# Moving the sums of w_out's features into the late local attention, and tying V's transposes to the next strip

## The chip, the cores and the metric

The kernel runs on one core of a Trainium2 chip. A core has five engines that each take their own instructions in order and wait for one another through semaphores: TensorE (PE, matrix products; its weight loads, PEld, overlap its products), VectorE (DVE), ScalarE (ACT), GpSimd (POOL) and SyncE (SP), which in this kernel issues every DMA. The metric is the device time of one execution in microseconds (us). Three executions of the kernel before gave 2171.97, 2172.36 and 2172.82 us; their median is 2172.36 us.

## The reference, cut to what matters

One encoder layer over two requests (a prompt of 1024 tokens, a sample of 256), each with 16 learned meta tokens in front:

```python
u = rms_norm(h, norm_w) @ w_in              # 2048 -> 6656 features
qa, ka, va, za, qb, kb, vb, zb = jnp.split(u, split_points(), axis=-1)
ya = global_gqa(rope(norm(qa)), rope(norm(ka)), va) * silu(za)      # 8 heads, 2 groups of K and V
yb = neighbourhood_attention(norm(qb), norm(kb), vb, rpb) * silu(zb)  # 8 local heads, 8 x 16 window
y = concatenate([ya, yb]) @ w_out           # 2048 -> 2048
return h + y
```

All is float32. A float32 product is made of three products in the type fp32r: a number is split into a high part h and a remainder l, and h·h, h·l and l·h are added.

## The kernel before

**Two chunks of tokens.** `chunk1` projects 512 tokens (the sample, the first 240 prompt tokens and the meta tokens) and runs the sample's attention. `chunk2` projects the other 784 prompt tokens in two blocks of 512 and 272 columns and runs the prompt's attention. `outproj` then multiplies with `w_out`.

**Strips.** w_in is cut into 52 strips of 128 features: Q, K, V and Z of the global heads and of the local heads. `project` takes one to three strips, `strips` (lines 184 to 227) runs them: for each of four quarters `c` of the 2048 input features it loads a piece of weights `wr` (line 196), splits it into `wh` on ACT and `wl` on DVE (lines 65 and 66), and runs for each block `b` of tokens 4 × 3 matmuls (lines 217 to 219). In `chunk2`, strips not named in `AGAIN` load their `wl` from HBM, where `chunk1` left it; the local heads 4 to 7 split again. When a strip is done, its `evac` brings it out of PSUM and norms it: K and Q through `qk_evac`, Z through `z_evac`, V through `v_rows` (line 279) and then transposes on PE against an identity (`v_turn`, line 286; `rows_out`, line 530), whose results ACT copies out of the only PSUM tile `tp` and SP stores to HBM (`vn`).

**Order.** The instructions are traced by the program and then placed on each engine's queue by a scheduler that follows a simulated timeline; on the chip each queue runs in just that order. `add_manual_dep(a, b.name, NoSync)` only puts `a` behind `b` in that order, and `issue_after(b)` does so for all instructions of a block on `b`'s engine. `turn_ins` (line 229) collects transposes in the list `turned`; in the kernel before only those of `chunk1`'s last V strip are put behind a matmul, the last of the first quarter and block of `chunk2`.

**Places.** After each odd quarter of a strip, `run_due` (line 233) takes the next entry of the list `due`. In `chunk2`, the first 8 local strips are spread over the global heads; the other 24 run after them and give 48 places (`LATE`), into which `local_heads` (line 899) puts the loads, the `scores` and, two places later, the `values` of the local heads 0 to 6; the last strip is local head 7's Z, and head 7's attention runs in the first places of `outproj`. Before the last strip, `turn` reverses the order of its blocks.

**Sums of w_out.** `outproj` multiplies by a scheme with seven products of halves of y and w_out instead of eight (Strassen's, in Winograd's form), which needs four sums of w_out's quarters. `w_sums` (line 579) is a generator with 16 rounds of two steps: step one loads four tiles `wq` of 128 × 512 from w_out (line 593), step two makes four differences on DVE (line 586, put behind the last split of weights) and stores them to `td` in HBM (line 603). `project` takes a step for each strip of `chunk1` from the 21st on. The tiles come from the pool `xr` (10 buffers), which also holds x while it is loaded. `outproj` reads `td` for its third product and later (line 1008).

**The passage from chunk1 to chunk2.** `load_all_x` (line 141) loads the x of `chunk2` into 16 tiles `xb` and 16 tiles `xa` (line 161, tile name `x`), which lie where `chunk1` had its own x; ACT and DVE scale and split them (lines 162 and 163). The last Q strip's store `qfd` (line 647) stands on SP's queue among these loads.

Of the kernel before, what the change touches and what calls it, by code (L numbers as in the profile page):

```python
# [12 lines left out]
F32 = mybir.dt.float32  # L13
# [8 lines left out]
P = 128  # L22
DM = 2048
KT = 16
# [34 lines left out]
class Kern:  # L59
# [88 lines left out]
    def load_all_x(self):  # L148


        nc, self.xload = self.nc, {}
        for kt in range(KT):
            w = self.nw[:, kt:kt + 1]
            self.xs[kt] = []
            ta = self.x.tile([P, 2, NB], F32R, tag="xa", name="x", align_bytes=ALIGN)
            tb = self.xb.tile([P, NX], F32R, tag="xb", name="xb", align_bytes=ALIGN)
            o = 0
            for h, l in ((ta[:, 0], ta[:, 1]), (tb[:, :NT2], tb[:, NX - NT2:])):
                r, n = l.bitcast(F32), l.shape[1]
                with self.tc.issue_after(self.early):  # L160
                    self.xload.setdefault(kt, nc.sync.dma_start(r, self.x2d[kt][:, o:o + n]).ins)
                nc.scalar.activation(h, r, AF.Copy, scale=w)
                nc.vector.scalar_tensor_tensor(out=l, in0=r, scalar=w, in1=h.bitcast(F32), op0=ALU.mult, op1=ALU.subtract)
                self.xs[kt].append((h, l))
                o += n
        self.behind = [None] + [self.xload[c] for c in range(WCH - 1, KT, WCH)]
        for d, c in self.consts:
            with self.tc.issue_after(self.xload[KT - 1]):
                nc.sync.dma_start(d, c)
# [12 lines left out]
    def strips(self, jobs, getx):  # L182


        nc, tc = self.nc, self.tc
        out = [[pool.tile([P, 512], F32, tag=tag, name="pp") for pool, tag in pools] for _, _, pools in jobs]
        for c in range(KT // WCH):
            ws = []
            behind = self.behind.pop(0) if self.behind else None
            for j, (s, _, _) in enumerate(jobs):  # L190
                wp = self.w if j < 2 else self.w1
                with tc.high_priority(offset=self.woff), tc.issue_after(behind) if behind else nullcontext():
                    w = self.raw.tile([P, WCH, P], F32, tag="raw", name="wr")
                    cuts = ((0, 1), (1, WCH)) if self.projected == 3 and c == 0 and not self.second else ((0, WCH),)
                    for i, e in cuts:
                        self.lastw = nc.sync.dma_start(w[:, i:e], self.io["w_in"][s][:, c * WCH + i:c * WCH + e, :]).ins
                    wh = wp.tile([P, WCH, P], F32R, tag="wh", name="wh")
                    wl = wp.tile([P, WCH, P], F32R, tag="wl", name="wl")
                    if self.second and s not in AGAIN:
                        nc.sync.dma_start(wl[:].bitcast(F32), self.wld[s][:, c * WCH:(c + 1) * WCH, :])  # L200
                        nc.scalar.copy(wh[:], w[:])
                    else:
                        for i, e in cuts:
                            self.lastsplit = self.split(wh[:, i:e], wl[:, i:e], w[:, i:e])
                            self.lasthi = self.hi
                ws.append((wh, wl))
                if not self.second and s not in AGAIN:
                    nc.sync.dma_start(self.wld[s][:, c * WCH:(c + 1) * WCH, :], wl[:].bitcast(F32))
            nb = len(jobs[0][1])
            for b in range(nb)[::-1] if self.turn else range(nb):  # L210
                for k in range(WCH):
                    kt = c * WCH + k
                    xh, xl = getx(kt)[b]
                    first, last = kt == 0, kt == KT - 1
                    for (wh, wl), ps, (_, blocks, _) in zip(ws, out, jobs):
                        p, n = ps[b], blocks[b][1]
                        nc.tensor.matmul(p[:, :n], wh[:, k, :], xh[:, :n], start=first, stop=False)  # L217
                        nc.tensor.matmul(p[:, :n], wh[:, k, :], xl[:, :n], start=False, stop=False)  # L218
                        self.lastmm = nc.tensor.matmul(p[:, :n], wl[:, k, :], xh[:, :n], start=False, stop=last).ins  # L219
                if self.second and self.turned:  # L220
                    for i in self.turned:
                        tc.add_manual_dep(i, self.lastmm.name, mybir.DependencyInfo(
                            mybir.DependencyClass.NoSync, mybir.DependencyReason.DATA), reason="turned")
                    self.turned = None
            if c % 2:
                self.run_due()
        return out

    def turn_ins(self, i):
        if not self.second:  # L230
            self.turned.append(i)

    def run_due(self):
        if self.late:
# [327 lines left out]
    def project(self, *parts):  # L562

        if not self.second:
            self.projected += len(parts)
            if self.projected > 20:
                for _ in range(len(parts)):
                    next(self.sums, None)
            kt = self.projected - 33
            for i in [i for i in self.xsq if i < kt]:  # L570
                self.square_x2(i, self.xsq.pop(i))
            if 0 <= kt < KT:
                with self.tc.issue_after(self.lastw):
                    self.xsq[kt] = self.load_x2(kt)
            if self.projected == 48:
                self.early = self.lastw
        jobs = [(p[0], p[1], [p[3] if len(p) > 3 else (self.pp, "pp")] * len(p[1])) for p in parts]
        out = self.strips(jobs, self.xs.__getitem__ if self.second else self.get_x)
        return [p[2](ps) for p, ps in zip(parts, out)]

    def w_sums(self):

        nc, w = self.nc, self.io["w_out"]

        def sub(out, a, b):
            nc.vector.tensor_tensor(out=out, in0=a, in1=b, op=ALU.subtract)

        for k in range(8):
            for o in range(0, FH, FB):
                q = {}  # L590
                for n, j, c in (("12", k, FH + o), ("11", k, o), ("22", 8 + k, FH + o), ("21", 8 + k, o)):
                    r = self.xr.tile([P, FB], F32, tag="xr", name="wq")
                    nc.sync.dma_start(r[:], w[:, j, c:c + FB])
                    q[n] = r[:]
                yield

                with self.tc.issue_after(self.lastsplit):
                    sub(q["11"], q["12"], q["11"])
                    sub(q["12"], q["22"], q["12"])
                    sub(q["22"], q["22"], q["11"])  # L600
                    sub(q["21"], q["22"], q["21"])
                for n, p in (("11", 5), ("12", 7), ("22", 6), ("21", 4)):
                    nc.sync.dma_start(self.td[p][:, k, o:o + FB], q[n])
                yield

    def chunk1(self):
        nc, io = self.nc, self.io
        self.early_due, self.place = {}, 0
        self.due, self.late, self.turn, self.behind, self.turned = iter(()), [], False, [], []
        self.woff, self.second, self.projected, self.sums = 0, False, 0, self.w_sums()  # L610
        self.scale2 = [self.one2.tile([P, T2], F32, tag=n, name=n) for n in ("rb2", "eb2")]
        self.xsq = {}
# [27 lines left out]
        def qb_strip(s, h, wc):  # L640
# [3 lines left out]
            def evac(ps):  # L644
                o, n = BQ
                self.qk_evac(ps[0], o, n, wc, None, [], q[:, :n])
                nc.sync.dma_start(self.qfd[h][:], q[:, NS:n])
                return q[:, :NS]
            return s, [BQ], evac

# [80 lines left out]
        for h in range(8):  # L731
# [9 lines left out]
                got["v"], = pr(vj)  # L741
                pr(zj)
            else:
                self.turned = []
                v, z = pr(v_strip(VB + h, 2 + h), z_strip(ZB + h, 8 + h))
                for _ in run(8 + h, q, z, k, *v, self.bias_table(h, "bs", (2 * HALF,))[:]):
                    pass
# [2 lines left out]
    def chunk2(self):  # L750
# [7 lines left out]
        self.consts = [(ct, io["ropec"][:, T1:]), (st, io["ropes"][:, T1:])]  # L758
        self.load_all_x()
        BL = [(0, NB), (NB, T2 - NB)]  # L760

        def k_first(g):
            t = self.k.tile([P, 2 * NP + 2 * NMETA], F32R, tag="k1", name="kf", align_bytes=ALIGN)
# [134 lines left out]

        def local_heads():
            places = [[] for _ in range(LATE)]  # L900
            seq = (values, load_v, load_z, scores, load_kq)

            def put(n, f, *a):
                places[n].append((seq.index(f), f, a))
# [1 line left out]
            for h in range(NH - 1):  # L906
# [4 lines left out]
                if h + 2 < NH:  # L911
                    put(max(o + 3, 8 * h - 2), load_kq, h + 1)
                    put(max(o + 5, 8 * h), load_v, h + 1)
                    put(max(o + 5, 8 * h), load_z, h + 1)
            put(LATE - 4, load_kq, NH - 1)
            put(LATE - 2, load_v, NH - 1)
            return [sorted(p, key=lambda x: x[0]) for p in places]

# [12 lines left out]
        for g in range(2):  # L931
            if g == 0:
                k, _ = pr(k_strip(KA, 0, kw, True), v_rows_of(VA, 0))
            else:
                k, = pr(k_strip(KA + g, g, kw, True))
                pr(v_rows_of(VA + g, g))
# [8 lines left out]
            f(0)  # L945
        self.due = iter(local_heads())
        fill(len(late) - 1)
        self.turn = True
        fill(1)
        load_z(NH - 1)  # L950
        self.due = iter([[(0, f, (NH - 1, b)) for f, b in ((values, n - 2), (scores, n)) if 0 <= b < 4] for n in range(6)])
# [360 lines left out]
```

## Time and profile before

| | |
|---|---|
| median of three executions | 2172.36 us |
| the profiled execution | 2171.32 us |
| its span, first to last instruction | 2169.5 us |
| ACT busy | 1119.3 us, 52% |
| POOL busy | 516.4 us, 24% |
| moved by DMA | 383.83 MB, 177 GB/s over the span |
| `chunk1`, by the first and last of its matmuls | to about 609 us |
| first score of the late local attention; end of the last strip | 1325.4 us; 1774.6 us |

An engine is busy while one of its instructions runs. Matmuls overlap: two matmuls of 128 × 512 start 0.23 us apart, though each is shown with 0.39 us. A row of the view of groups or of the timeline gives line, engine, operation and tiles as out<-in, and in brackets the idle time of the engine just before, with what ended it. A row of the view of waits reads: engine, tile, line <- what it waited for: us in total, times, the longest. A row of the view by stretches gives the stretch's length and, for each engine, busy time and count, then TensorE's granted clock as a share of full speed, the DMA engines' busy share and GB/s.

### The profile page before, as it was taken

How to read it: one execution, taken by the hardware profiler on the slowest of the kernel's cores; microseconds unless marked ns; L12 is line 12 of the kernel's file. 1: busy time of each engine (PE TensorE's matmuls, PEld its weight loads, DVE VectorE, ACT ScalarE, POOL GpSimd, SP SyncE). 2: the span in 40 equal slices, each digit the busy share in tenths (PEclk: the TensorE clock that was granted, in tenths of full speed). 3: DMA queues.
4: the chain of work that ended last, by engine and by line, in shares of the span. 5: the costliest groups of instructions: out<-in, count | busy, mean ns of one | idle time of the engine just before them, and what ended most of it. 6: DMA issues, size and time to landing. Idle time of an engine off the chain costs nothing. (4 is left out here: it accounts for less than half of the span.)

```text
span 2169.5 us, 34094 instructions
## 1 busy us (share of the span) xinstructions
PE 2155.3 (99%) x11745; PEld 1877.3 (87%) x11745; DVE 1644.9 (76%) x2989; ACT 1119.3 (52%) x2291; POOL 516.4 (24%) x250
## 2 busy tenths in 40 slices
PE   9999999999999999999999999999999999999999
PEld 7888878888888999999999999898999888888887
DVE  7787886777874899987799988677787876545763
ACT  6555544555554676665666765444443454232230
POOL 1232331221311233322143314333333311000000
PEclk9999999999999999999999999999999999999999
DMA  8767798988654333334333344554433364662663
GB/s 300 223 203 227 237 307 302 339 277 270 214 191 148 100 105 113 118 110 142 100 107 109 105 129 151 184 156 138 135 127 119 113 206 147 238 227 99 233 223 107
DMA packets 263182, 383.83 MB, mean 177 GB/s; under 512 B 44992, under 2 KB 112992, under 8 KB 263008
## 3 DMA queue, kind: packets, MB, share of 16 engines
q1 hardware_dynamic: 263008, 381.65, 53.8%
q8 instruction: 92, 1.51, 0.3%
q14 instruction: 82, 0.67, 0.1%
HBM read 281.01 MB, written 100.38 MB: 176 GB/s over the span
## 5 line engine op out<-in xcount | busy, mean ns | idle before, releaser
L217 PE MATMUL pp<-x,wh 128*128 128x512 f32 (+1 forms) x1664 | 654.8, 395 | 2.7 <-ACT wh L65 1.6
L219 PE MATMUL pp<-x,wl 128*128 128x512 f32 (+1 forms) x1664 | 649.4, 391 | 1.1 <-DVE wl L66 1.1
L218 PE MATMUL pp<-x,wh 128*128 128x512 f32 (+1 forms) x1664 | 648.9, 390 | 0.0
L219 PEld LDWEIGHTS pp<-x,wl 128*128 128x128 f32 x1664 | 313.0, 188 | 63.1 <-DVE wl L66 2.4
L217 PEld LDWEIGHTS pp<-x,wh 128*128 128x128 f32 x1664 | 312.8, 188 | 59.7 <-ACT wh L65 3.9
L218 PEld LDWEIGHTS pp<-x,wh 128*128 128x128 f32 x1664 | 313.2, 188 | 52.6
L253 POOL PARTITION_ALL_REDUCE m<-ms x78 | 224.1, 2873 | 408.4 <-ACT ms L251 400.4
L66 DVE TENSOR_TENSOR wl<-wr,wh 128x512 fp32r<-128x512 f32 (+2 forms) x287 | 219.2, 766 | 112.9 <-ACT wh L65 102.2
L336 POOL PARTITION_ALL_REDUCE tot<-a x80 | 182.4, 2280 | 451.2 <-DVE a L333 451.2
L65 ACT CAST wh<-wr 128x512 fp32r<-128x512 f32 (+2 forms) x287 | 174.2, 611 | 201.9 <-PE pp L218 177.2
L218 PE MATMUL pp<-xb,wh 128*128 128x272 f32 x832 | 240.1, 289 | 0.0
L219 PE MATMUL pp<-xb,wl 128*128 128x272 f32 x832 | 239.6, 288 | 0.0
L217 PE MATMUL pp<-xb,wh 128*128 128x272 f32 x832 | 239.6, 288 | 0.0
L1036 PE MATMUL pq<-wm,yh 128*128 128x512 f32 x560 | 218.6, 390 | 0.0
L1037 PE MATMUL pq<-wm,yh 128*128 128x512 f32 x560 | 218.0, 389 | 0.0
L1038 PE MATMUL pq<-wm,yl 128*128 128x512 f32 x560 | 217.9, 389 | 0.0
L318 POOL PARTITION_ALL_REDUCE ma<-m x80 | 103.3, 1291 | 400.2 <-DVE m L316 399.7
L217 PEld LDWEIGHTS pp<-xb,wh 128*128 128x128 f32 x832 | 156.5, 188 | 7.4
L218 PEld LDWEIGHTS pp<-xb,wh 128*128 128x128 f32 x832 | 156.4, 188 | 7.4
L219 PEld LDWEIGHTS pp<-xb,wl 128*128 128x128 f32 x832 | 157.3, 189 | 0.3
L1038 PEld LDWEIGHTS pq<-wm,yl 128*128 128x128 f32 x560 | 105.1, 188 | 22.0
L1036 PEld LDWEIGHTS pq<-wm,yh 128*128 128x128 f32 x560 | 105.1, 188 | 21.6
(211 smaller groups left out, 3835.3 us busy)
## 6 DMA issues: line engine op xcount, KB each, us to landing
wr<-in_w_in SPq DMA_DIRECT2D x413, 256.0 KB, 3.5
wld<-wl SPq DMA_DIRECT2D x132, 256.0 KB, 4.2
wl<-wld SPq DMA_DIRECT2D x132, 256.0 KB, 3.2
yr<-yd SPq DMA_DIRECT2D x35, 512.0 KB, 5.5
wq<-in_w_out SPq DMA_DIRECT2D x64, 256.0 KB, 5.0
td<-wq SPq DMA_DIRECT2D x64, 256.0 KB, 4.4
ww<-td SPq DMA_DIRECT2D x64, 256.0 KB, 5.4
ww<-in_w_out SPq DMA_DIRECT2D x48, 256.0 KB, 4.5
```

Source lines behind the costliest of these rows:

```text
L65: self.hi = nc.scalar.copy(hi, full).ins
L66: return nc.vector.tensor_tensor(out=lo, in0=full, in1=hi.bitcast(F32), op=ALU.subtract).ins
L217: nc.tensor.matmul(p[:, :n], wh[:, k, :], xh[:, :n], start=first, stop=False)
L218: nc.tensor.matmul(p[:, :n], wh[:, k, :], xl[:, :n], start=False, stop=False)
L219: self.lastmm = nc.tensor.matmul(p[:, :n], wl[:, k, :], xh[:, :n], start=False, stop=last).ins
L253: nc.gpsimd.partition_all_reduce(m2[:], ms[:], P, RED.add)
L318: nc.gpsimd.partition_all_reduce(ma[:], m1[:], P, RED.max)
L336: nc.gpsimd.partition_all_reduce(tot[:], a1[:], P, RED.add)
L1036: nc.tensor.matmul(ps, yh, wh, start=k == 0, stop=False)
L1037: nc.tensor.matmul(ps, yh, wl, start=False, stop=False)
L1038: self.lastmm = nc.tensor.matmul(ps, yl, wh, start=False, stop=k == 7).ins
```

## The change

Three things change. The 32 steps of `w_sums` leave `project` and go into the places 6 to 37 of the late local attention, last in each place, and their tiles come from the pool `ph` (tags `ph` and `pl`, two buffers each), which the global attention used for its probabilities. All transposes of V, in both chunks, are put behind a matmul of the next strip: the last one of the quarter and block that `tie` names, (1, 0) in `chunk1`, (0, 0) at `chunk2`'s start, (0, 1) after its first project and (1, 0) in its last strip. And the store `qfd` of `chunk1`'s last Q strip is put behind the load of x's ninth tile on SP's queue.

```diff
@@ load_all_x
+        self.tc.add_manual_dep(self.qstore, self.xload[KT // 2].name, mybir.DependencyInfo(
+            mybir.DependencyClass.NoSync, mybir.DependencyReason.DATA), reason="x first")
         self.behind = [None] + [self.xload[c] for c in range(WCH - 1, KT, WCH)]
@@ strips
-                if self.second and self.turned:
+                if self.turned and (c, b) == self.tie:
                     for i in self.turned:
                         tc.add_manual_dep(i, self.lastmm.name, mybir.DependencyInfo(
                             mybir.DependencyClass.NoSync, mybir.DependencyReason.DATA), reason="turned")
-                    self.turned = None
+                    self.turned = []
...
     def turn_ins(self, i):
-        if not self.second:
-            self.turned.append(i)
+        self.turned.append(i)
@@ project
             self.projected += len(parts)
-            if self.projected > 20:
-                for _ in range(len(parts)):
-                    next(self.sums, None)
@@ w_sums
-                    r = self.xr.tile([P, FB], F32, tag="xr", name="wq")
+                    r = self.ph.tile([P, FB], F32, tag="ph" if n in ("12", "22") else "pl", name="wq", align_bytes=ALIGN)
                     nc.sync.dma_start(r[:], w[:, j, c:c + FB])
@@ chunk1
-        self.due, self.late, self.turn, self.behind, self.turned = iter(()), [], False, [], []
+        self.due, self.late, self.turn, self.behind, self.turned, self.tie = iter(()), [], False, [], [], (1, 0)
...
-                nc.sync.dma_start(self.qfd[h][:], q[:, NS:n])
+                self.qstore = nc.sync.dma_start(self.qfd[h][:], q[:, NS:n]).ins
...
-                self.turned = []
                 v, z = pr(v_strip(VB + h, 2 + h), z_strip(ZB + h, 8 + h))
@@ chunk2
         BL = [(0, NB), (NB, T2 - NB)]
+        self.tie = 0, 0
...
-            seq = (values, load_v, load_z, scores, load_kq)
+            seq = (values, load_v, load_z, scores, load_kq, next)
...
             put(LATE - 4, load_kq, NH - 1)
+            for n in range(32):
+                put(6 + n, next, self.sums)
...
                 k, _ = pr(k_strip(KA, 0, kw, True), v_rows_of(VA, 0))
+                self.tie = 0, 1
...
-        self.turn = True
+        self.turn, self.tie = True, (1, 0)
         fill(1)
```

## The prediction

> **What bounds the kernel now.** I read the page's head first, then the view of waits for PE, then busy time by stretches.
>
> ```profile
> span 2169.5 us, 34094 instructions
> PE 2155.3 (99%) x11745; PEld 1877.3 (87%) x11745; DVE 1644.9 (76%) x2989; ACT 1119.3 (52%) x2291; POOL 516.4 (24%) x250
> ...
> PE tp L530 <- DVE vt L279: 2.9, 2, 2.5
> ...
> PE tp L286 <- DVE vt L279: 1.3, 1, 1.3
> ...
> PE pp L219 <- DVE wl L66: 1.1, 2, 0.6
> PE pp L217 <- ACT x L162: 1.1, 1, 1.1
> PE po L408 <- ACT ph L65: 1.1, 2, 0.5
> ```
>
> PE is busy for all but 2169.5 − 2155.3 = 14.2 us, and the change gives PE not one matmul more or less. So no faster engine elsewhere can help: the change can only win what PE stands idle or slowed, and can only lose by making it wait anew. The stretches say where it stands.
>
> ```profile
> 216.00:285.00 69.00, 65.44 (x307) 53.42 (x307) 59.95 (x104) 36.82 (x76) 27.52 (x10) 1.00 0.75 245
> 285.00:600.00 315.00, 315.00 (x1428) 260.40 (x1428) 243.26 (x410) 160.11 (x325) 74.55 (x29) 1.00 0.85 282
> 600.00:625.00 25.00, 23.92 (x119) 19.47 (x118) 22.81 (x42) 17.41 (x35) 3.22 (x2) 1.00 0.70 248
> 705.00:1340.00 635.00, 635.00 (x4115) 581.40 (x4114) 560.62 (x1022) 423.98 (x866) 187.70 (x91) 1.00 0.36 113
> 1359.00:1680.00 321.00, 320.87 (x1925) 289.15 (x1924) 244.02 (x522) 143.60 (x329) 111.68 (x59) 1.00 0.45 144
> 1761.60:1765.10 3.50, 3.50 (x11) 2.76 (x10) 1.69 (x3) 1.46 (x4) 0.00 (x0) 0.51 0.78 253
> ```
>
> Three spots stand out: 216 to 285 (idle 69.00 − 65.44 = 3.56 us), the passage to chunk 2 (25.00 − 23.92 = 1.08 us), and about 1752 to 1765, where the two waits of `tp` L530 sum to 2.9 us and the granted clock then falls to 0.51.
>
> **The last strip (V's tie).** The transposes of the last V strip stand early in the last Z strip.
>
> ```profile
> 1753.34 0.32 SPq L856 DMA_DIRECT2D qfull<-q2d  x1
> ...
> 1756.87 1.05 ACT L65 CAST q<-qfull 128x1024 fp32r<-128x1024 f32 x1 [2.00 <-DMA vm<-vmd]
> ...
> 1757.95 1.23 DVE L66 TENSOR_TENSOR q<-qfull,q 128x1024 fp32r<-128x1024 f32 x1 [2.09 <-ACT q L65]
> ...
> 1760.03 0.43 DVE L279 TENSOR_TENSOR vt<-pp,rb 128x272 f32<-128x272 f32 x1
> ...
> 1752.97 0.66 PE L530 MATMUL tp<-ident,vt 128*128 128x128 f32 x4 [0.41 <-DVE vt L279]
> ...
> 1757.74 0.29 PE L219 MATMUL pp<-xb,wl 128*128 128x272 f32 x1
> 1757.86 0.28 PE L217 MATMUL pp<-xb,wh 128*128 128x272 f32 x1
> 1760.61 0.52 PE L530 MATMUL tp<-ident,vt 128*128 128x128 f32 x3 [2.46 <-DVE vt L279]
> ...
> 1761.95 0.63 PE L218 MATMUL pp<-x,wh 128*128 128x512 f32 x1
> 1762.38 0.63 PE L219 MATMUL pp<-x,wl 128*128 128x512 f32 x1
> ```
>
> A load of head 7's q lands late, ACT splits it, DVE's half of that split waits 2.09 us, and `vt` is queued behind it; PE waits 2.46 us. Then starts of 128x512 matmuls lie 0.43 us apart instead of 0.23: 3.4 us at half the clock cost 1.7 us. Together 2.9 + 1.7 = 4.6 us. With the tie (1, 0) all seven transposes come behind the second quarter's last matmul. From 1757.86 PE has 6 matmuls of 272 columns (0.12 us apart) and 12 of 512 (0.23) to go, 3.5 us, and it comes about 0.8 us earlier, as the first four transposes (some 0.4) and their wait (0.41) are gone from in front: about 1760.5, and `vt` ends at 1760.03 + 0.43 = 1760.46. I leave 0.2 us of wait and take −4.4. Bounds: −4.6, and 0 if the lateness goes on to the first products of w_out, which use the same `tp` tile and whose operands then have 4.4 us less lead.
>
> The Trainium skill (TensorE: Matmul & The Clock Gate, the table of states in Part 1 and "Why this matters for your kernels") gives the half clock as the state after an idle window of about 3.4 us. The 2.46 us here stood right before it, so the trace differs in the length. By the page's length the half clock would have another cause and stay; this step would be worth −2.7, and the sum below −5.8.
>
> **The sums leave chunk 1.** Removed there: 64 loads, 64 subtractions, 64 stores.
>
> ```profile
> wq<-in_w_out SPq DMA_DIRECT2D x64, 256.0 KB, 5.0
> td<-wq SPq DMA_DIRECT2D x64, 256.0 KB, 4.4
> ...
> L586 DVE TENSOR_TENSOR wq<-wq x64: 673/684/2730, 237.1 to 582.5; 128x512 f32<-128x512 f32 x64
> ...
> L586 DVE TENSOR_TENSOR wq<-wq 128x512 f32<-128x512 f32 x64 | 50.7, 792 | 0.5
> ...
> 266.45 1.41 DVE L586 TENSOR_TENSOR wq<-wq 128x512 f32<-128x512 f32 x2
> ...
> 268.37 0.69 DVE L586 TENSOR_TENSOR wq<-wq 128x512 f32<-128x512 f32 x1
> ...
> 269.31 0.68 DVE L586 TENSOR_TENSOR wq<-wq 128x512 f32<-128x512 f32 x1
> ...
> 270.25 0.67 DVE L66 TENSOR_TENSOR wl<-wr,wh 128x512 fp32r<-128x512 f32 x1
> ```
>
> One round is four subtractions, 4 × 0.684 = 2.7 us, and here all four stand in the 3.8 us before a split of weights; PE's waits for `wl` (1.1 us in two) and for `vt` (1.3 us) follow within ten microseconds and are each under 2.7 us. So they go, the last one by its tie as well. The waits for `ph` (1.1 us in two) come from ACT; I keep half. 3.56 − 0.55 gives −3.0; bounds −3.6 and, should the list come out in another order with as many stalls, 0.
>
> **x first.** On SP's queue the store of Q stands between the last `xb` loads and the first `x` load:
>
> ```profile
> 591.99 3.93 SPq L161 DMA_DIRECT2D xb<-x2d  x8
> 604.18 0.32 SPq L647 DMA_DIRECT2D qfd<-qs  x1
> 604.59 1.82 SPq L161 DMA_DIRECT2D x<-x2d  x4
> ...
> L855 SPq DMA_DIRECT2D qfull<-qfd x8: 422/432/666, 636.9 to 1737.1; - x8
> ```
>
> From 595.9 to 604.2 SP waits for Q's norm (8.2 us). The store then goes behind the ninth `x` load, so the first loads start up to 8 us earlier, and PE's 1.1 us wait for `x` L162 ends: −1.1, bounds −1.1 and 0. Behind the store nothing else is urgent: what it stores is the last to be read again, at 1737.1.
>
> **The sums arrive in the late local attention.** The matmul of `values` with `Pm` comes first in place 6 and, for local heads 0 to 6, last in place 45:
>
> ```profile
> 1358.96 0.41 PE L506 MATMUL po<-Pm,vm 128*128 128x256 f32 x1
> ...
> 1749.23 0.42 DVE L328 TENSOR_TENSOR Pm<-Sm,Pm 16x256 fp32r<-16x256 f32 x1
> ...
> 1750.56 0.28 PE L506 MATMUL po<-Pm,vm 128*128 128x256 f32 x1
> ```
>
> (1750.56 − 1358.96) / 39 = 10.0 us a place, so the 32 steps cover about 1359 to 1680. DVE's share there, 244.02 / 321 = 0.76, becomes (244.02 + 50.7) / 321 = 0.92. The nearest row is the global attention: 560.62 / 635 = 0.88 with PE busy throughout. DMA gains 128 × 0.256 MB in 321 us, some 105 GB/s, to about 250 GB/s, under the 282 of 285 to 600, where PE did not idle. The chain with the least lead is a block's probabilities: between `Pm`'s end at 1749.65 and its use at 1750.56 0.9 us remain, against a round of 2.7 us; but that is a head's last block, and the scheduler knows of the rounds and moves `values` behind them. Bounds: 0 (the rows of 285 to 600, which held most of the 16 rounds without an idle PE) and +43.8 (16 × 2.74, nothing hidden). I take +0.8, nearest to the first row. The other ties (a V strip in chunk 1 or 2 with its transposes some 4 to 5 us later) have a wait of PE nowhere and readers strips later: 0, bounds 0 and +0.5, a wait for `tp` between the two groups. The `wq` loads have four buffers in place of ten, so each round's loads wait on SP for the stores before. Before, such waits were
>
> ```profile
> SPq L593 <- DMA td<-wq: 8.0, 7, 2.2
> SPq L196 <- DVE wl L66: 182.4, 115, 6.4
> ```
>
> at most 2.2 us, and SP stands waiting for free weight buffers for 182.4 us anyway, so it runs ahead of need: +0.2, bounds 0 and 15 × 2.2 = 33 us, if nothing covers them.
>
> **Sum.** −4.4 − 3.0 − 1.1 + 0.8 + 0.2 = −7.5 us, against the profiled execution's 2171.32 (span and 1.8 us around it): 2163.8. That execution lies 1.0 us under the median of three, so the median after is 2172.4 − 7.5 = **2164.9 us**.
>
> A rule that speaks against this: the Trainium skill (Advanced Engine Details and Errata, "VectorE Performance Modes") says that VectorE's second SBUF port is shared with GpSimd, so that the two block each other. The trace agrees: a subtraction took 2.73 us at worst against 0.684, 0.792 on average. GpSimd is busy 111.68 / 321 = 0.35 of the new stage against 74.55 / 315 = 0.24 of the old, and an estimate by that rule stretches the 64 subtractions by 64 × 0.108 × 0.35 / 0.24 = 10 us instead of 7; by this sum 3 us of DVE, hidden as the rest.
>
> **Rivals.** (a) The last strip's stall only moves. The q split that makes `vt` late is untouched, and PE now reaches w_out's products earlier; `tp` or their operands end last. Then −3.0 − 1.1 + 1.0 = −3.1: 2169.3. For it speaks that `vt` ends within 0.1 us of the new point. (b) Slower: the rounds break the lead of `values`. Places 6 to 37 hold the `values` of 22 blocks; if the 10 that are third or fourth of their head each wait 2.7 − 0.9 = 1.8 us, that is +18 in place of +0.8, so net +9.7: 2182. It decides once DVE runs more than 0.9 us behind the scheduler's timeline at a `Pm`. Against it: in the global attention DVE at 0.88 never held PE, though 0.92 lies above that row. (c) SP: a fifth of the 33 us reaches PE, +7 in place of +0.2: 2172. Against it stand the waits for free buffers. (d) The change does not do what it says: a tie is only a lower bound in a queue, and the order made for the sums gives new waits as large as those removed: 2172.
>
> **Chances.** Forecast 0.56 (own range 2161.5 to 2168), (a) 0.17, (b) 0.14, (c) 0.08, (d) 0.05. About 0.2%, 4.3 us, is what a measurement tells from no change. Faster is the forecast with a third of (a) and a little of (c): 0.63; same 0.23; slower 0.14. The low end is all bounds of gain (9.3 us) and 1.5 us for runs; the high end takes in (a), (c), (d) and leaves (b): 2161.5 to 2174.
>
> **What would show it.** PE's list of waits without `tp` L530, `tp` L286, `wl` L66 and `x` L162; no stretch with a clock of 0.5 near 1760; `qfd` L647 behind nine `x` loads; L586 between 1359 and 1690 with PE idle under 1 us there. Wrong it is if PE waits for `Pm`, `S` or `wl` in that stretch, if SP's `wq` loads stand before late `wr` loads, or if the first products wait for `tp` or `wm`.

## The result, and the profile after

| | before | after |
|---|---|---|
| median, us | 2172.36 (2171.13 to 2173.37, 19 runs) | 2177.08 (2172.06 to 2178.96, 19 runs) |
| ratio to before, with its 95% interval | | 1.0020 [1.0014, 1.0027] |
| span of the profiled execution, us | 2169.5 | 2176.9 |

The changed kernel is slower by 4.7 us; 2164.9 was predicted, and the range ended at 2174.0. First the head of the page after, then PE's list of waits (line, what it waited for: us in all, times, longest).

```profile
span 2176.9 us, 34089 instructions
...
PE 2157.5 (99%) x11745; PEld 1879.8 (86%) x11745; DVE 1643.3 (75%) x2989; ACT 1115.7 (51%) x2291; POOL 531.2 (24%) x250
```

```profile
PE tp L531 <- DVE vt L280: 5.0, 2, 3.7
PE po L507 <- DVE Pm L329: 2.4, 3, 1.2
PE po L409 <- ACT ph L65: 1.5, 2, 1.3
...
PE tp L287 <- DVE vt L280: 1.1, 1, 1.1
PE pp L219 <- ACT x L162: 1.1, 1, 1.1
```

PE's idle time rose from 14.2 to 2176.9 − 2157.5 = 19.4 us, and its busy time for the same 11745 matmuls by 2.2: 5.2 us of new waiting, and some matmuls at a lower clock. `vt`, `x` and `ph` are still in the list, and `Pm` is new. Busy time by stretches after says where (columns: stretch, us, PE, PEld, DVE, ACT, POOL, granted clock, DMA share, GB/s):

```profile
216.00:285.00 69.00, 65.43 (x312) 54.37 (x311) 58.42 (x104) 39.77 (x82) 25.63 (x11) 1.00 0.62 198
600.00:625.00 25.00, 23.92 (x120) 19.81 (x119) 19.37 (x35) 15.66 (x30) 3.22 (x2) 1.00 0.59 196
1359.00:1680.00 321.00, 317.25 (x1890) 285.70 (x1890) 278.62 (x574) 140.05 (x320) 119.06 (x59) 0.99 0.74 240
1387.90:1391.30 3.40, 3.40 (x11) 2.72 (x10) 1.74 (x6) 1.26 (x3) 1.37 (x2) 0.50 1.08 393
1777.00:1780.40 3.40, 3.40 (x12) 2.83 (x11) 2.90 (x6) 2.73 (x8) 0.00 (x0) 0.50 1.10 383
```

In the first two spots, where 3.0 and 1.1 us were to be won, PE idles as long as before: 3.57 (3.56) and 1.08 (1.08) us. The late local attention lost: idle 3.75 us where it was 0.13, and a half-clock stretch at 1387.9 that costs 1.7 more, 5.3 in all. The half clock of the last strip is still there, 15 us later. The timeline of the late local attention after, in the first round of the sums and around its worst spot:

```profile
1355.81 0.69 DVE L584 TENSOR_TENSOR wq<-wq 128x512 f32<-128x512 f32 x1 [3.76 <-DMA wq<-in_w_out]
...
1379.10 0.69 DVE L584 TENSOR_TENSOR wq<-wq 128x512 f32<-128x512 f32 x1 [2.83 <-DMA wq<-in_w_out]
1379.71 0.42 DVE L350 TENSOR_TENSOR y<-po,z 128x256 f32<-128x256 f32 x1
1380.82 0.69 DVE L584 TENSOR_TENSOR wq<-wq 128x512 f32<-128x512 f32 x1 [0.69 <-DMA wq<-in_w_out]
...
1384.30 0.68 DVE L280 TENSOR_TENSOR vt<-pp,rb 128x512 f32<-128x512 f32 x1
...
1385.04 0.44 PE L531 MATMUL tp<-ident,vt 128*128 128x128 f32 x2 [1.31 <-DVE vt L280]
...
1386.14 0.41 DVE L329 TENSOR_TENSOR Pm<-Sm,Pm 16x256 fp32r<-16x256 f32 x1
...
1386.70 0.36 PE L507 MATMUL po<-Pm,vm 128*128 128x256 f32 x1 [1.23 <-DVE Pm L329]
```

VectorE works in order. It stands 3.76, 2.83 and 0.69 us for loads of `wq`; the evacuation `vt` and the probabilities `Pm`, which need nothing of the sums, stand behind these subtractions, and at 1385 PE waits for both. One line of the view of the tile `wq` gives all that VectorE stood for these loads, and one of the waits of SP's queue what SP, which issues them, stood for the stores of the round before.

```profile
  DMA wq<-in_w_out: 7.7, 4
```

```profile
SPq L591 <- DMA td<-wq: 36.0, 34, 3.7
```

Before, SP's wait for stores was 8.0 us in 7 pieces. The two do not fall together, though. VectorE's four waits are over by 1401, and by then SP had stood 6.7 of the 36.0 us for stores. The longest of the four, 3.76 us, comes in the first round: its four loads were issued by 1351.6, and the first store `td` only at 1353.5.

### The profile page after: what moved, and what is told of

It reads as the page before. It is cut to its first block, busy times and chain, and to the rows that moved or that the text cites. A ratio compares the mean times of both kernels' runs of the same rounds, so it can differ in the third digit from the quotient of the medians.

```text
span 2176.9 us, 34089 instructions
## 1 busy us (share of the span) xinstructions
PE 2157.5 (99%) x11745; PEld 1879.8 (86%) x11745; DVE 1643.3 (75%) x2989; ACT 1115.7 (51%) x2291; POOL 531.2 (24%) x250
## 4 chain that ended last, share of the span: by engine, by line
PE 88%; DVE 5%; DMA 3%; ACT 1%; issue 1%; SPq 1%; POOL 1%; DVEq 0%; POOLq 0%; ACTq 0%
PE pp L219 19%; PE pp L221 19%; PE pp L220 19%; PE pq L1039 6%; PE pq L1037 6%; PE pq L1038 6%; PE sp L369 1%; PE sp L368 1%; PE sp L370 1%; PE po L409 1%; PE po L411 1%; PE po L410 1%; PE sp L476 1%; PE po L510 1%; DMA td<-wq 1%
## 5 line engine op out<-in xcount | busy, mean ns | idle before, releaser
L254 POOL PARTITION_ALL_REDUCE m<-ms x78 | 232.0, 2975 | 396.0 <-ACT ms L252 354.2
L66 DVE TENSOR_TENSOR wl<-wr,wh 128x512 fp32r<-128x512 f32 (+2 forms) x287 | 224.1, 784 | 124.7 <-ACT wh L65 115.9
L337 POOL PARTITION_ALL_REDUCE tot<-a x80 | 186.8, 2336 | 479.6 <-DVE a L334 478.2
```

Of the source, the lines that this page charges most:

```text
L66: return nc.vector.tensor_tensor(out=lo, in0=full, in1=hi.bitcast(F32), op=ALU.subtract).ins
L254: nc.gpsimd.partition_all_reduce(m2[:], ms[:], P, RED.add)
L337: nc.gpsimd.partition_all_reduce(tot[:], a1[:], P, RED.add)
```

## The experiments

All runs are compared with runs of the kernel before on the same chip; its median was between 2171.5 and 2172.1 us each time.

**Which part of the change costs.** Two kernels: the change without the sums' move, and the move alone.

e1_sums_home, against the kernel after:

```diff
             self.projected += len(parts)
+            if self.projected > 20:
+                for _ in range(len(parts)):
+                    next(self.sums, None)
...
-                    r = self.ph.tile([P, FB], F32, tag="ph" if n in ("12", "22") else "pl", name="wq", align_bytes=ALIGN)
+                    r = self.xr.tile([P, FB], F32, tag="xr", name="wq")
...
-            for n in range(32):
-                put(6 + n, next, self.sums)
```

> The changed kernel with the sums back in the first chunk, in their old tiles; the ties and the store behind x's loads stay. Theory (the sums' stay in the late local attention costs PE the waits at 1383 to 1388, 1447 and 1510, about 4.7 us, and one window of half clock, 1.7 us): 2171 us, those waits gone, the last strip's wait for vt (3.7 us and 1.7 us of clock) still there. Rival (the ties cost it, in every strip): 2176 or more.

e2_sums_only is the same edit the other way round, on the kernel before.

> The kernel before with the sums alone moved; no new ties, the store of Q in its old place. Theory: the late local waits of the changed kernel come back (DVE waits for wq loads) and the last strip is as before (2.5 us and the clock): 2172.4 + 5 = 2177 or so; in the first chunk the waits at 250 to 285 stay within 1 us of 3.5 although the subtractions are gone, since DVE is full there without them. Rival (the subtractions made those waits): 2174, with PE idle under 1 us there.

e1 measured 2172.12 us, 1.0003 [0.9994, 1.0011]; e2 2176.3 us, 1.0023 [1.0014, 1.0033]. The move is the cost, and what the ties and x's order do together is not told from nothing. In e1 PE idles nowhere from 1359 to 1680. Its last strip came out other than expected: PE waited 2.6 us there and no half clock followed, where the changed kernel lost 3.7 us and a half clock; e2's, without the ties, lost 2.8 us, also without one. The waits of e2, PE's and VectorE's:

```profile
PE tp L530 <- DVE vt L279: 6.1, 3, 3.3
PE po L506 <- DVE Pm L328: 1.6, 2, 1.0
...
DVE wq L583 <- DMA wq<-in_w_out: 9.1, 4, 4.2
```

In e2 no subtraction is left in the first chunk, and PE idles from 216 to 285 as long as before, 3.48 us (3.56). The waits for `vt` and `ph` stay, 1.3 us each; the two for `wl` are gone, and one of 0.6 us for `qs` and one of 0.3 us for `Pm` are new. In e1 all ties stand and the subtractions are back: the two waits for `wl` are back too, and `vt` still takes 1.1 us.

**When the sums run.** e3_sums_late, against the kernel after: `put(16 + n, ...)` for `put(6 + n, ...)`, so that they begin 100 us later.

> The changed kernel with the 32 steps in the places 16 to 47 instead of 6 to 37, where each strip splits its weights on DVE, so that every round of subtractions stands behind a split of its own place. Theory (in places 6 to 15 nothing ties the rounds, they run ahead, and DVE waits in its queue for loads that wait for the stores): DVE's waits for wq fall from 7.7 us to under 2 and PE's waits at 1383 to 1510 go: 2171 to 2172. Rival (DVE's share of over 0.85 is what hurts, wherever the rounds are): 2176 or more, with waits of PE for Pm between 1450 and 1760.

e3: 2174.39 us, 1.0012 [1.0003, 1.0020]. VectorE waits for no `wq` and the spot at 1383 is clean, but more than half of the price stays, 2.9 us over before: PE's `po` L507 waits 5.8 us in three pieces for `Pm`, at 1504, 1692 and 1754, and a half clock follows the last. So VectorE's waits for the loads are one way in which the move costs, and not the only one.

e7_anchored, against the kernel after, puts the subtractions behind the last VectorE instruction of each `put_y`:

```diff
-        nc.vector.scalar_tensor_tensor(out=y[:], in0=y[:], scalar=-1.0, in1=r[:], op0=ALU.mult, op1=ALU.mult)
+        last = nc.vector.scalar_tensor_tensor(out=y[:], in0=y[:], scalar=-1.0, in1=r[:], op0=ALU.mult, op1=ALU.mult).ins
+        if self.second:
+            self.lastsplit = last
```

> The changed kernel with every round of subtractions put behind the last DVE instruction of the latest values (or the latest split of weights), so that the rounds can't run ahead of their places in the strips that split no weights. Theory: DVE's waits for wq loads fall from 7.7 us to under 2, PE's waits at 1383 to 1388 and the half clock go; waits for Pm of a head's last block may stay: 2172.5 to 2174.5. Rival (running ahead is not what hurts): 2176 or more with the waits at 1383 to 1388.

e7: 2190.92 us, 1.0083 [1.0070, 1.0095]. My theory that the place in VectorE's order was the fault fell: the waits at 1383 went, but VectorE then stood 14.7 us in 6 pieces for `wq`, and PE 12.1 us for `Pm`.

e13_halves, on the same anchor, cuts the sums into pieces of 256 columns in alternating halves of the four tiles, each loaded one step ahead:

```diff
-                    r = self.ph.tile([P, FB], F32, tag="ph" if n in ("12", "22") else "pl", name="wq", align_bytes=ALIGN)
+        H = FB // 2
+        def part(i, n):
+            return q[n][:, H * (i % 2):H * (i % 2) + H]
...
+        load(0)
+        yield
+        for i, (k, o) in enumerate(pieces):
+            if i + 1 < len(pieces):
+                load(i + 1)
```

> The changed kernel with the sums in pieces of 256 columns, in alternating halves of the same four tiles, each piece loaded one place ahead of its subtractions, and the subtractions behind the last VectorE instruction of put_y in that place: as much data, twice as many instructions (128 subtractions, 128 loads, 128 stores). Theory (VectorE stands in order for wq loads, SyncE for td stores): no VectorE wait for wq over 1 us, no SyncE wait for td stores over 2 us, and 2172 to 2174 in spite of twice the instructions. Rival (the work and the bytes cost, not the waits): 2175 to 2180.

e13: 2199.27 us, 1.0127 [1.0113, 1.0141]; a miss as a test, since the waits did not go but grew. Waits of PE, VectorE and SP:

```profile
PE po L509 <- DVE Pm L329: 14.4, 6, 4.9
...
DVE wq L586 <- DMA wq<-in_w_out: 24.8, 10, 6.6
...
SPq L613 <- DVE wq L586: 24.8, 30, 3.2
SPq L599 <- DMA td<-wq: 21.9, 26, 2.6
```

SP too works in order: L613 issues the stores, which wait for the subtractions, and the next loads stand behind them. A load written a step earlier still stood behind the stores of the step before.

**Which part of the sums costs.** Five kernels: the kernel before, sums where they were, with extra work in places 6 to 37. e5_more_subs has 64 subtractions on four tiles loaded once; e11_more_subs_set sets these tiles in place of the load; e6_more_dma has 64 loads and 64 stores; e14_loads_subs loads and subtractions; e15_subs_stores subtractions and stores. What they compute is used nowhere. The core of the edit (e14):

```diff
+                    nc.sync.dma_start(t[:], w[:, k + 8 * (i // 2), FH * (i % 2) + o:][:, :FB])
+                    q.append(t)
+                yield
+                with self.tc.issue_after(self.lastsplit):
+                    for a, b, c in ((1, 0, 1), (0, 2, 0), (2, 2, 1), (3, 2, 3)):
+                        nc.vector.tensor_tensor(out=q[a][:], in0=q[b][:], in1=q[c][:], op=ALU.subtract)
+                yield
...
+            for n in range(32):
+                put(6 + n, next, more)
```

> The kernel before, its sums where they were, and in the places 6 to 37 of the late local attention 64 more subtractions of 128x512 on four tiles that are loaded once: the moved work of DVE without its DMAs. Results of the added work are not used. Theory (the price is DVE's queue standing still for loads, and loads of the next head's k and q landing later; the subtractions alone find room): within 1.5 us of before, PE idle under 1.5 us from 1359 to 1680. Rival (DVE's work is the price): 2176 or more, PE waiting for Pm and vt there.

> The kernel before, its sums where they were, and in the places 6 to 37 64 more loads from w_out and 64 more stores to HBM of the same tiles, without a subtraction: the moved DMAs alone. The stored tiles are not read. Theory (the loads count through DVE's waiting in its queue for them, and here no engine waits for them): within 1.5 us of before, though the loads of k land later than the 3.8 us of before and ACT's waits for kfull grow above 15.5 us. Rival (DMA traffic and SP's waits for landings are the price by themselves): 2175 or more.

> The kernel before with 64 more subtractions of 128x512 in the same places of the late local attention, on four tiles that VectorE sets once and nothing loads or stores (their results are used nowhere). Theory (the subtractions as mere work cost nothing; what cost 2 us in the run with loaded tiles was the one wait for that load): 2171 to 2173, ratio 0.9995 to 1.0005, no new TensorE wait over 1 us between 1350 and 1400. Rival (VectorE's work itself costs): 2174 to 2175 as with the loaded tiles.

> The kernel before with 64 more loads of 128x512 and the 64 subtractions on them in the same places of the late local attention, nothing stored. Theory (VectorE's wait for the loads is the larger part): 2174.5 to 2177, VectorE's wait for wx transfers 5 us or more. Rival (the stores are): 2172 to 2174, since without stores a tile is free as soon as its subtraction is done and the next load is early.

> The kernel before with 64 more subtractions on four tiles set once, each followed by a store to scratch as in the sums (64 stores), nothing loaded. Theory (loads are the larger part): 2172.5 to 2174.5, about the 1.1 us of the subtractions alone and little more. Rival (the stores are the larger part): 2174.5 to 2177, with SyncE or VectorE waiting for the scratch stores to land.

| run | added | median, us | ratio to before | VectorE's wait for these loads, us |
|---|---|---|---|---|
| e11 | subtractions | 2173.17 | 1.0007 [0.9998, 1.0016] | none |
| e15 | subtractions, stores | 2173.78 | 1.0010 [1.0001, 1.0019] | none (2.7 for stores) |
| e5 | subtractions, one load of four tiles | 2174.34 | 1.0012 [1.0003, 1.0021] | 4.0, 1 |
| e6 | loads, stores | 2174.76 | 1.0012 [1.0003, 1.0021] | none |
| e14 | loads, subtractions | 2176.35 | 1.0020 [1.0011, 1.0029] | 5.8, 4 |
| e2 | all three, the sums' move | 2176.30 | 1.0023 [1.0014, 1.0033] | 9.1, 4 |

The 43.8 us of VectorE work cost about 1 us, which is not told from none. Loads and subtractions together (e14), where VectorE waits for a transfer, have a median as far over before as the whole move's, with nothing stored. The profile bears this out in part only: from 1359 to 1680 PE idles 2.5 us in e14, but 2.7 us in e15 as well (before: 0.1), and 2.1 of the 5.5 us by which e14's span is longer come from a wait for `ph` at 254, in code that the edit leaves as it was. The intervals of neighbouring rows overlap, and even those of the first row and the last touch; the order of the rows between them is not shown.

**ScalarE's waits for the next head's k and q.** e6 lost at 1385 because ScalarE stood 8.38 us for a `kfull` load, with the copy `vl` that PE needed behind it. e9_cast_late, on the kernel before, takes such waits away: the casts of kfull and qfull stand one place behind their loads. e10_after_cast_late does it on the kernel after.

```diff
+        def cast_kq(h):
+            k, tab, qf = kqs[h]
+            with self.tc.issue_after(self.lastr) if h else nullcontext():
+                kqs[h] = k_cast(k), tab, q_cast(qf)
...
+                    put(max(o + 3, 8 * h - 2) + 1, cast_kq, h + 1)
...
+            put(46, cast_kq, NH - 1)
```

> The kernel before with one change: in the late local attention the ScalarE casts and VectorE subtractions that read the next head's kfull and qfull tiles stand one place (one strip of the schedule) behind the loads that they read, and behind the last reciprocal of that place. Theory (engines that work in order stand for transfers that land later than the schedule took them): ScalarE's idle time ended by kfull transfers, 15.5 us in 6 pieces, falls under 5 us; the last strip's TensorE wait of 2.46 us and the 1.7 us of half clock behind it go, because VectorE is no longer held there by ScalarE's cast of qfull: 2167 to 2169.5, ratio 0.998 to 0.999. Rival (TensorE waits there for the VectorE copies that stand in that order anyway): 2171 to 2173, the wait stays over 2 us.

> The changed kernel with the same one change: casts of kfull and qfull one place behind their loads. The sums still move. If what ScalarE loses for kfull is the larger part of the sums' price: 2170.5 to 2173, no TensorE wait over 1 us for Pm behind a kfull wait. If VectorE's waits for the wq transfers (7.7 us in 4 pieces) are the larger part: the waits at 1383 to 1388 stay, 2174 to 2177.

e9: 2171.17 us, 0.9995 [0.9986, 1.0004]; e10: 2178.55 us, 1.0030 [1.0020, 1.0040]. ScalarE's wait for `kfull`, 15.5 us before, is gone from e9's list, and the time does not tell; in e10 it is gone as well and the time is no better, with VectorE still waiting 6.5 us for `wq`. These waits are not what the move costs.

**The last strip, and x.** Each of the next five moved what the run before showed to be late. e4_vt_first, on the kernel after: both `vt` traced ahead of the transposes.

```diff
-                for p, (o, n) in zip(ps, BL):
-                    self.rows_out(self.v_rows(p, o, n), n, self.vn[g], C1P + o)
+                vts = [self.v_rows(p, o, n) for p, (o, n) in zip(ps, BL)]
+                for vt, (o, n) in zip(vts, BL):
+                    self.rows_out(vt, n, self.vn[g], C1P + o)
```

> The changed kernel with both vt of a V strip in the second chunk traced before the first block's transposes. Theory (the second vt takes its turn on DVE only after the first block's transposes, which the tie moved to 1767, and so falls behind the weights of w_out): both vt come within 2 us of each other in all V strips, PE's 3.7 us wait near 1772 and the half clock after it go, 2172 to 2173. Rival (the one PSUM tile of the transposes, whose copy on ACT came at 1775, holds PE as long): the wait stays over 2 us with vt long done, 2176 or more.

e4: 2179.65 us, 1.0041 [1.0027, 1.0054]. Both `vt` were done by 1762 and PE's wait for `vt` is gone, so their order was its cause. PE now waited for the copy `vl`, 2.0 us, without a half clock. The late local attention lost more than in after: 4.0 us for `Pm` at 1442 and 6.8 us at half clock. The profile is of e4's fastest execution, 4 us under its median, and does not show the rest.

e8_home_mend: sums home, e4's edit, the second block's transposes one quarter later in the last strip, and the first `x` cast of the second chunk ahead of the `Sm` copy:

```diff
+                if kt == 0 and o == 0:
+                    self.tc.add_manual_dep(self.lastsm, cast.name, mybir.DependencyInfo(
+                        mybir.DependencyClass.NoSync, mybir.DependencyReason.DATA), reason="cast first")
...
+                if self.turned and (c, b) == (2, 0) and self.turn:
+                    for i in self.turned[4:]:
```

> The changed kernel with the sums back in the first chunk, both vt of a V strip in the second chunk ahead of its transposes, in the last strip the second block's transposes one quarter later than the first's, and ACT's cast of chunk 2's first x ahead of the copy of the last sample scores (with the store of Q behind x's loads). Theory (the last strip's wait is vt behind the first transposes, then the one PSUM tile; x's wait is the order of two instructions on ACT): waits for tp in the last strip under 0.5 us, no half clock there, no wait for x L162: 2167 to 2168. Rival (the operands of w_out's first products end last once PE comes earlier): 2170 or more, with waits of pq.

e12_best is e8 with the later casts of e9.

> All that the runs so far point to, together: sums back in the first chunk, both V rows traced ahead of the transposes, the second row's transposes of the last strip one quarter later, the second chunk's first x cast ahead of the Sm copy, and casts of kfull and qfull one place behind their loads. Theory: the last strip's wait of 3.7 us for a copy that ScalarE does late, and its half clock, go with ScalarE's waits for kfull: 2164 to 2168, ratio 0.997 to 0.9985. Rival (ScalarE's copy stands late for another cause): 2169 to 2171.5 like the run without the later casts.

e8: 2170.47 us, 0.9993 [0.9984, 1.0002]; e12: 2170.14 us, 0.9992 [0.9983, 1.0001]. PE's wait for `x` is gone from both lists; in the last strip PE waited 3.7 and 2.3 us for `vl`, in e8 with a half clock behind it. The last strip's wait only moved.

e16_best2 leaves the ties of the kernel before, and has its x loads first, the `x` cast first, and the later casts, those of the last head behind the second `vt`:

```diff
+        self.lastr = self.lastvt
+        cast_kq(NH - 1)
```

> The kernel before with three orders changed and nothing else: x's loads ahead of the first chunk's last store of q, the second chunk's first x cast ahead of the Sm copy, and the casts of kfull and qfull one place behind their loads, those of the last head behind the second vt of the last V strip. Theory: TensorE's wait of 1.1 us for x goes (0.7 to 1.1), and the last strip's wait of 2.4 us for vt with its 1.7 us of half clock: 2167 to 2169, ratio 0.9975 to 0.9988. Rival (another wait takes the last strip's place, as in the three runs that moved it): 2170 to 2172.

e16: 2171.12 us, 1.0000 [0.9992, 1.0009], a miss: PE still waited 2.59 us there. Its timeline, ScalarE and VectorE, shows why:

```profile
1756.19 1.05 ACT L65 CAST q<-qfull 128x1024 fp32r<-128x1024 f32 x1 [2.27 <-DMA qfull<-q2d]
1757.14 0.61 ACT L65 CAST wh<-wr 128x512 fp32r<-128x512 f32 x1
...
1757.79 0.69 DVE L66 TENSOR_TENSOR wl<-wr,wh 128x512 fp32r<-128x512 f32 x1 [2.88 <-DMA ww<-in_w_out]
...
1759.19 0.43 DVE L284 TENSOR_TENSOR vt<-pp,rb 128x272 f32<-128x272 f32 x1
```

The bound held VectorE's half of the split back, but not ScalarE's cast. That stood 2.27 us for its load, the cast `wh` behind it, VectorE's `wl` behind `wh` (the row names `ww`, but starts 0.04 us after `wh` ends, at 1757.14 + 0.61), and `vt` behind `wl`. e17_best3 binds to ScalarE's copies instead:

```diff
+            self.lastvl = nc.scalar.copy(t[:, :f, :], tp[:, :f, :]).ins
...
+        self.lastr = self.lastvl
```

> The kernel before with x's loads ahead of the last store of q, the first x cast ahead of the Sm copy, casts of kfull and qfull one place behind their loads, and those of the last head behind ScalarE's copies of the last V strip. Theory (ScalarE standing for qfull is the cause of the last strip's wait): no TensorE wait over 1 us at 1750 to 1765, no half clock there, 2166.5 to 2169, ratio 0.9975 to 0.9988. Rival (VectorE stands there for something else): 2170 to 2172 with the wait in place.

e17: 2169.88 us, 0.9993 [0.9984, 1.0002], its profiled span 2166.4. PE's two longest waits, and two rows of its timeline:

```profile
PE pq L1055 <- ACT yh L65: 2.3, 1, 2.3
PE po L413 <- ACT ph L65: 1.6, 2, 1.0
```

```profile
1752.93 0.60 ACT L65 CAST wh<-wr 128x512 fp32r<-128x512 f32 x1
...
1755.33 0.43 DVE L284 TENSOR_TENSOR vt<-pp,rb 128x272 f32<-128x272 f32 x1
```

`vt` comes 4.7 us earlier than before (1760.03), PE waits for neither `tp` L535 nor `x`, and no half clock is left but that of the program's end. e16 and e17 differ in that one bound, which settles the cause of the last strip's stall. The time gives back some of it: a wait of 2.3 us for `yh` appears in the output stage, and the interval still touches 1. No version is shown to beat the kernel before.

e18_best3_sums is e17 with the sums moved, from place 16 on.

> The same kernel with the sums moved to the late local attention, from place 16 on, where an earlier run had no VectorE wait for wq. If the move costs only through its waits: within 1 us of the run without the sums. If the work and the transfers have a price of their own: 1.5 to 3 us more than the run without the sums.

e18: 2176.67 us, 1.0021 [1.0012, 1.0030]: 6.8 us over e17, more than expected on either side, and VectorE's list has no wait for `wq`. PE's longest wait, and the timeline of GpSimd and VectorE at its second spot, ahead of 1629:

```profile
PE po L511 <- DVE Pm L333: 7.6, 4, 3.5
```

```profile
1619.62 5.62 POOL L341 PARTITION_ALL_REDUCE tot<-a  x1 [8.53 <-DVE a L338]
1625.14 1.14 POOL L323 PARTITION_ALL_REDUCE ma<-m  x1
...
1626.32 0.43 DVE L501 TENSOR_TENSOR S<-S,ma 128x256 f32<-128x256 f32 x1 [2.40 <-POOL ma L323]
...
1629.10 0.41 DVE L333 TENSOR_TENSOR Pm<-Sm,Pm 16x256 fp32r<-16x256 f32 x1
```

A block's probabilities are one chain through VectorE (`m`), GpSimd (`ma`), VectorE (`S`), ScalarE and VectorE (`Pm`). GpSimd's sum of the block before took 5.62 us, where the median of this run is 2.2, `ma` stood behind it, and VectorE idled 2.40 us at the head of the rest of the chain. That a chain without slack breaks here without any wait for `wq` is shown; that the subtractions made the sum begin late or last long was not tried by itself.

## Why the prediction was wrong

**The last strip, −4.4: the step "`vt` ends at 1760.46" failed.** It took the row of before for a `vt` whose place in VectorE's order the tie changed. The last strip after, by VectorE, ScalarE and PE:

```profile
1759.21 0.67 DVE L280 TENSOR_TENSOR vt<-pp,rb 128x512 f32<-128x512 f32 x1
...
1774.46 0.62 ACT L65 CAST wm<-ww 128x512 fp32r<-128x512 f32 x1 [1.12 <-DMA ww<-in_w_out]
...
1775.12 0.69 DVE L66 TENSOR_TENSOR wm<-ww,wm 128x512 fp32r<-128x512 f32 x1 [1.04 <-ACT wm L65]
1775.72 0.43 DVE L280 TENSOR_TENSOR vt<-pp,rb 128x272 f32<-128x272 f32 x1
...
1766.99 0.60 PE L531 MATMUL tp<-ident,vt 128*128 128x128 f32 x4
1776.30 0.52 PE L531 MATMUL tp<-ident,vt 128*128 128x128 f32 x3 [3.68 <-DVE vt L280]
```

The program writes the second `vt` behind the first block's transposes, which the tie put at 1766.99. So it now stands on VectorE behind the splits of the first products' weights, which wait for a transfer. In e1, with the same tie, it came late in the same way; in e4, written first, it did not. PE waits 3.68 us once instead of 0.41 and 2.46, and the half clock follows: about +0.8 in place of −4.4. That is rival (a), which put this step at 0 and was somewhat too kind. The loads that made `vt` late in the kernel before were named rightly, and e17 shows it.

**The first chunk, −3.0: the step "So they go" failed.** It counted each wait that goes as won. The two waits for `wl` (1.1 us) and the second for `ph` (0.55) did go with the subtractions, in after and in e2. But PE then stood for the next operand that was late: `qs` (0.84), `Pm` (0.28) and longer for `ph` at 254 (1.35 in place of 0.52). `vt` took 1.1 us with its tie and 1.3 without it (e2), so the subtractions were not its cause. The sum stayed, 3.57 us in place of 3.56. VectorE is about as busy there without the subtractions, 58.42 of 69 us against 59.95. How much of it is the chance of one execution is open: the wait for `ph` at 254 was 0.7 us in e6 and 2.6 us in e14, whose first chunk is that of the kernel before.

**x first, −1.1: right about SP, wrong about what ends last.** The first four loads did move up; PE waited 1.1 us as before, since the cast stands on ScalarE behind a copy that waits for PE. SP's and ScalarE's timelines after:

```profile
594.26 1.84 SPq L161 DMA_DIRECT2D x<-x2d  x4
...
605.47 0.42 SPq L645 DMA_DIRECT2D qfd<-qs  x1
...
608.33 0.38 ACT L425 ACTIVATE Sm<-sm_ps 48x256 f32<-48x256 f32 x1 [6.17 <-PE sm_ps L423]
608.61 1.94 ACT L162 ACTIVATE x<-x,nw 128x512 fp32r<-128x512 f32 x3
```

With the cast ahead of that copy (e8, e12, e16, e17) the wait is gone.

**The late local attention, +0.8 and +0.2: mis-sized; the profiles say +5.3.** The work itself was costed nearly rightly (e11: +1.1 us for 43.8 us of it, not told from none). What failed is "the scheduler knows of the rounds and moves `values` behind them", and the sum had no term for VectorE standing in order for a load: on the chip it stood 7.7 us for `wq`, with `vt` and `Pm` behind it. Why these loads came late is not settled. SP's wait for stores, with four buffers in place of ten, is not enough to explain it: the loads behind the longest wait were issued before any store was, in e14 VectorE stood 5.8 us with nothing stored, and in e3 and e18 SP stood over 42 us for stores and VectorE for no `wq`. Rival (b) named the place where PE would wait, `Pm`. In after its lead was lost to VectorE's waits; in e3 and e18 it was lost without them, and how is open but for the chain shown above. Rival (c) named SP, but the way that the trace shows led through VectorE.

Of the 7.4 us between the two profiled spans, the late local attention (+5.3) and the last strip (+0.8) make 6.1; the first chunk's spot and x make none. In the medians after lies 4.7 us over before, and e2, the move alone, 4.8. The 4.1 us between after and e1 are not the late local attention's alone, since e1's last strip lost less with the same ties.

## What to carry to other kernels

Work moved to a stage where every engine has spare time is not cheap for that alone. On an engine that works in order, one instruction that stands for a transfer holds back all that needs nothing of it, so ask of each moved instruction what it waits for and who is queued behind it, before its duration. Even where no moved instruction waited for its load, the move cost 6.8 us (e18 over e17). To end a wait, follow the whole chain of queues back to the transfer at its head and move the instruction that stands for that transfer; four edits that moved a later link only moved the wait. And a wait that goes is not yet a gain: take the work out and see what the engine waits for next.

## What the runs showed of the hardware

How long PE stood still didn't decide by itself whether the half clock followed. Before, a wait of 2.46 us was followed by one stretch of about 3.4 us at 0.50; one of 2.2 us in e9 and one of 1.8 us in e12 (for `ph`, at 255) were too. After waits of 2.6 us (e1), 2.4 us (e15) and 2.3 us (e12 and e17, late in the kernel) none came. In after, two waits of 1.31 and 1.23 us within two microseconds were followed by one. The Trainium skill (TensorE: Matmul & The Clock Gate, Part 1, the table of states) puts the half clock after at least one idle window of about 3.4 us. The slow stretches here have that length; the idle time ahead of them was shorter in before, in e9, in e12 and at 1388 in after, so here the measurement decides. Two such stretches in a row, 6.8 us, followed longer stalls in e2, e13 and e18.

GpSimd's reduction of `tot` had a median of 2.0 us in the late local attention before and after, but single ones took 5.62 us (e18) and 4.86 us (e17). What stretches them wasn't tried.
